# Modulation columns of a hybrid attention, SSD and convolution kernel: from TensorE products over eight channel tiles to ScalarE products and GpSimd sums

## The chip, the core and the metric

The kernel runs on one core of a Trainium2 chip. Its metric is the time of one execution on the device in microseconds. A core has TensorE (PE in the rows; PEld are its weight loads), VectorE (DVE), ScalarE (ACT), GpSimd (POOL) and SyncE (SP), each with its own queue that runs in order, and 16 DMA engines.

## What is computed

Two layers of a diffusion backbone with 512 latent tokens and 256 context tokens of 1024 channels. Each layer normalizes its input and modulates it with a shift and a scale, projects it once for three branches (attention, a bidirectional state space scan, a convolution module), merges the branches and adds the result through a gate:

```python
mod = jax.nn.silu(c) @ w_mod + b_mod
mod_c = jax.nn.silu(c_ctx) @ w_mod + b_mod
shift, scale, gate = jnp.split(mod[:, None, :], 3, axis=-1)
shift_c, scale_c, gate_c = jnp.split(mod_c, 3, axis=-1)
h = rmsnorm(x, norm_w) * (1.0 + scale) + shift
hc = rmsnorm(xc, norm_w) * (1.0 + scale_c) + shift_c
...
x_new = x + gate * out
...
return x_new, xc + gate_c * out_c
```

The change is about `mod` and `mod_c`: for each layer a vector of 1024 inputs times a matrix of 1024 x 3072, for two inputs (`c` and `c_ctx`). The matrix is 12.6 MB in each layer.

## The kernel before

**Layout.** Channels lie on the 128 partitions, tokens along the free axis; the 1024 channels are 8 tiles of 128. The 3072 modulation columns of a layer are 24 tiles of 128, written `m0`: 0 to 7 shift, 8 to 15 scale, 16 to 23 gate. Products of large matrices are done in three passes (`mm_cm_steps`, L175, and `mm_tm`, L216 to L218): a weight tile `raw` is split by ScalarE into `whi` (L156) and by VectorE into `wlo` (L157), the input stands split as `hh` and `hl`, and TensorE adds hi x hi, hi x lo and lo x hi. Weights pass through a ring of three `raw` tiles and five halves each of `whi` and `wlo`; SP issues the loads.

**Order in a layer.** First the gated inputs of the convolution module (`ps_u`, `ps_g`), then the projections `kvd`, `xbc` (8 tiles, each with a short convolution of 5 taps on VectorE, `xacc`, L564 and L567), `z` and `q`. Beside these VectorE works through the long convolution: 4 channel tiles with 31 taps, 30 of them on VectorE (`vacc`, L445), each adding `vt` times a tap to the sum in place. After `q` stands `layer_norm`, whose transposes (`pt_ln`, L617) read the finished taps of all four channel tiles. Then come the projections `gcv`, the scan with the merge of branch 2 woven in, attention with the merge of branch 1 woven in, the merge of branch 0, and the output projection (`ps_o`). In layer 0 that projection ends with the normalization for layer 1, which needs layer 1's shift and scale.

**Who sets the order.** From `kvd` to the end of attention TensorE runs in the order in which the code is written (`manual_schedule`). The other engines, and TensorE elsewhere, run in an order that the framework's scheduler makes before the run. An engine executes its list strictly in order, and a wait holds up all that stands behind it.

**The modulation.** The 16 column tiles of shift and scale of layer 0 come first (`mod_tiles`, L229) and are not touched. The remaining 32 (gate of layer 0 in the `xbc` stage, all of layer 1 in the three merges of layer 0) go through `Mods.visit` and `mod_half`. One visit treats 4 column tiles and half of the 8 channel tiles: two loads of 512 KB into the ring of weights, and 16 matmuls with the two input vectors as a stationary operand of 32 columns, the four column tiles in four column groups of the array:

```python
T.matmul(ps[32 * j:32 * j + 32, 0:P], sc[:, 4 * half + i, :], raws[i // 2][:, j, i % 2, :],
         start=(i == 0), stop=(i == 3), tile_position=(0, 32 * j))
```

The first half's result is copied out by ScalarE, the second half's is added by VectorE (L262), and a transpose on TensorE (L266) and an addition of the bias (L267) bring it into `mod`. `then` places the transpose about 12288 columns of matmul later.

Of the kernel before, what the change touches and what calls it, by code (L numbers as in the profile page):

```python
# [9 lines left out]
F32 = mybir.dt.float32  # L10
F32R = mybir.dt.float32r
AF = mybir.ActivationFunctionType
ALU = mybir.AluOpType
# [37 lines left out]
MOD_LAG = 12288  # L51
# [6 lines left out]
def hybrid_kernel(ctx, tc, xT, cc, consts, rope, mod_params, params, fnw, w_mod, w_cm, w_q, w_kvd, w_z,  # L58
# [71 lines left out]
    V.memset(nhalf, -0.5)  # L130

# [112 lines left out]
    def mod_half(li, mod, m0, half, part):  # L244


        raws = []
        for i in range(2):
            raw = wp.tile([P, 4, 2, P], F32, tag="raw", name="raw")
            k0 = 4 * half + 2 * i  # L250
            with tc.high_priority(offset=TOP):
                nc.sync.dma_start(raw, w_mod[li, m0:m0 + 4, :, k0:k0 + 2, :].rearrange("m p k c -> p m k c"))
            raws.append(raw)
        ps = pot("ps_mod")
        for i in range(4):
            for j in range(4):
                T.matmul(ps[32 * j:32 * j + 32, 0:P], sc[:, 4 * half + i, :], raws[i // 2][:, j, i % 2, :],
                         start=(i == 0), stop=(i == 3), tile_position=(0, 32 * j))
        if half == 0:
            S.activation(part, ps[:, 0:P], AF.Copy)  # L260
            return None
        V.tensor_tensor(out=part, in0=ps[:, 0:P], in1=part, op=ALU.add)  # L262

        def finish():
            pt = ps[:, P:2 * P]
            T.transpose(pt, part, ident)  # L266
            V.tensor_tensor(  # L267
                out=mod[:, m0:m0 + 4, :], in0=pt.rearrange("p (j r) -> p j r", j=4)[:, :, 0:2],
                in1=pmod[:, li, O_BMOD + m0:O_BMOD + m0 + 4].unsqueeze(2).to_broadcast([P, 4, 2]), op=ALU.add)

        return finish

    class Mods:


        def __init__(self, li, mod, m0):
            self.li, self.mod, self.m0, self.n = li, mod, m0, 0

        def visit(self):
            g, half = divmod(self.n, 2)  # L280
            if half == 0:
                self.part = sm.tile([P, P], F32, tag="part", name="part4")
            self.n += 1
            return mod_half(self.li, self.mod, self.m0 + 4 * g, half, self.part)
# [88 lines left out]
    for li in range(2):  # L373
# [168 lines left out]
        for ct in range(8):  # L542
# [15 lines left out]
            if li == 0 and ct % 2 == 1:  # L558
                fn = gate_mods.visit()
                if fn is not None:  # L560
                    soon.append(fn)
# [762 lines left out]
```

## Time and profile before

| what | value |
|---|---|
| time, median of 3 runs | 1486.73 us (1482.37 to 1487.7) |
| the profiled execution, its own time | 1484.83 us |
| its span in the trace | 1483.0 us |
| TensorE busy | 1441.4 us, 97% of the span |
| VectorE busy | 1038.6 us, 70% |
| ScalarE busy | 714.9 us, 48% |
| GpSimd busy | 80.4 us, 5% |
| mean granted TensorE clock, share of full | 0.994 |

Matmuls overlap in the pipeline, so a busy TensorE is counted from the start of the first to the end of the last, and distances of starts tell what one costs. VectorE's rows overlap a little too: an instruction is counted until its result is written. Busy shares are means over stages with different limits.

### The profile page before, as it was taken

How to read it: one execution, taken by the hardware profiler on the slowest of the kernel's cores; microseconds unless marked ns; L12 is line 12 of the kernel's file. 1: busy time of each engine (PE TensorE's matmuls, PEld its weight loads, DVE VectorE, ACT ScalarE, POOL GpSimd, SP SyncE). 2: the span in 40 equal slices, each digit the busy share in tenths (PEclk: the TensorE clock that was granted, in tenths of full speed). 3: DMA queues.
4: the chain of work that ended last, by engine and by line, in shares of the span. 5: the costliest groups of instructions: out<-in, count | busy, mean ns of one | idle time of the engine just before them, and what ended most of it. 6: DMA issues, size and time to landing. Idle time of an engine off the chain costs nothing.

```text
span 1483.0 us, 24837 instructions
## 1 busy us (share of the span) xinstructions
PE 1441.4 (97%) x9660; PEld 1251.2 (84%) x9660; DVE 1038.6 (70%) x1895; ACT 714.9 (48%) x1600; POOL 80.4 (5%) x177
## 2 busy tenths in 40 slices
PE   6999999999998999999999999999999999999997
PEld 5899899988887888888788888989988887888796
DVE  5689998766657776555444478899877788666564
ACT  5423543365444466556322344454464647666341
POOL 0000010100001210000000000001010121000000
PEclk9999999999999999999999999999999999999999
DMA  9223333223334323323554433223423242222551
GB/s 377 75 70 95 105 124 111 75 61 100 101 114 133 120 86 120 108 68 118 199 168 156 164 117 113 69 66 114 142 70 114 96 155 86 98 90 79 171 171 58
DMA packets 79671, 172.58 MB, mean 116 GB/s; under 512 B 7616, under 2 KB 37440, under 8 KB 79552
## 3 DMA queue, kind: packets, MB, share of 16 engines
q1 hardware_dynamic: 79552, 170.98, 35.1%
q8 instruction: 76, 1.25, 0.4%
q14 instruction: 43, 0.35, 0.1%
HBM read 143.43 MB, written 27.53 MB: 115 GB/s over the span
## 4 chain that ended last, share of the span: by engine, by line
PE 90%; DMA 3%; ACT 3%; DVE 2%; issue 1%; SPq 0%; POOL 0%; POOLq 0%; DVEq 0%; ACTq 0%
PE ps_gm L175 22%; PE ps_br L175 11%; PE ps_xbc L175 8%; PE ps_o L175 6%; PE ps_gcv L175 4%; PE ps_u L175 4%; PE ps_g L175 4%; PE po_v L1088 3%; PE ps_ga L175 3%; PE pt_p L1074 3%; PE ps_l L1028 2%; PE ps_z L216 1%; PE ps_q L217 1%; PE ps_z L217 1%; PE ps_q L216 1%; PE ps_z L218 1%
## 5 line engine op out<-in xcount | busy, mean ns | idle before, releaser
L156 ACT ACTIVATE whi<-raw 128x512 fp32r<-128x512 f32 (+1 forms) x316 | 198.7, 632 | 270.6 <-PE ps_gm L175 59.1
L157 DVE TENSOR_TENSOR wlo<-raw,whi 128x512 fp32r<-128x512 f32 (+1 forms) x316 | 217.2, 691 | 147.5 <-ACT whi L156 137.7
L445 DVE SCALAR_TENSOR_TENSOR vacc<-vt,par,vacc 128x783 f32<-128x783 f32 (+1 forms) x232 | 206.7, 891 | 8.9 <-ACT vacc L442 5.4
L175 PE MATMUL ps_gm<-hh,whi 128*128 128x512 f32 (+1 forms) x576 | 212.1, 368 | 0.0
L175 PE MATMUL ps_gm<-hh,wlo 128*128 128x512 f32 (+1 forms) x576 | 209.7, 364 | 0.0
L175 PE MATMUL ps_gm<-hl,whi 128*128 128x512 f32 (+1 forms) x576 | 209.0, 363 | 0.0
L175 PEld LDWEIGHTS ps_gm<-hh,wlo 128*128 128x128 f32 x576 | 109.0, 189 | 15.9 <-issue 2.1
L175 PEld LDWEIGHTS ps_gm<-hh,whi 128*128 128x128 f32 x576 | 109.1, 189 | 15.5 <-issue 2.0
L175 PEld LDWEIGHTS ps_gm<-hl,whi 128*128 128x128 f32 x576 | 108.9, 189 | 14.2 <-issue 1.0
L175 PE MATMUL ps_xbc<-hh,whi 128*128 128x512 f32 (+1 forms) x240 | 83.4, 348 | 0.0
L175 PE MATMUL ps_xbc<-hl,whi 128*128 128x512 f32 (+1 forms) x240 | 82.3, 343 | 0.0
L175 PE MATMUL ps_xbc<-hh,wlo 128*128 128x512 f32 (+1 forms) x240 | 82.3, 343 | 0.0
L1080 ACT ACTIVATE pth<-pt_p 128x512 f32<-128x512 f32 x72 | 43.5, 604 | 55.5 <-PE pt_p L1074 55.3
L698 ACT ACTIVATE tg<-ps_gm,hw 128x512 f32<-128x512 f32 x72 | 44.3, 615 | 47.6 <-PE ps_gm L175 46.5
L175 PE MATMUL ps_o<-yh,whi 128*128 128x256 f32 (+1 forms) x208 | 65.8, 318 | 0.5 <-DVE xnew L1153 0.3
L175 PE MATMUL ps_o<-yh,wlo 128*128 128x256 f32 (+1 forms) x208 | 65.7, 316 | 0.0
L175 PE MATMUL ps_o<-yl,whi 128*128 128x256 f32 (+1 forms) x208 | 65.7, 316 | 0.0
L1034 DVE TENSOR_REDUCE mx<-ps_l 128x1 f32<-128x512 f32 x64 | 43.9, 689 | 30.1 <-PE ps_l L1028 29.6
L567 DVE SCALAR_TENSOR_TENSOR xacc<-xraw,par,xacc 128x770 f32<-128x770 f32 (+1 forms) x64 | 62.7, 989 | 1.7 <-ACT xacc L564 1.5
L728 DVE SCALAR_TENSOR_TENSOR tg<-tg,ps_br 128x512 f32<-128x512 f32 x66 | 39.5, 599 | 32.7 <-PE ps_br L175 28.6
L1074 PE MATMUL pt_p<-mr,pe 128*128 128x128 f32 x416 | 62.3, 272 | 0.0
L1074 PEld LDWEIGHTS pt_p<-mr,pe 128*128 128x128 f32 x416 | 50.7, 140 | 10.5 <-issue 0.2
(281 smaller groups left out, 3635.7 us busy)
## 6 DMA issues: line engine op xcount, KB each, us to landing
raw<-in_w_cm_dram SPq DMA_DIRECT2D x96, 512.0 KB, 3.6
raw<-in_w_mod_dram SPq DMA_DIRECT2D x32, 512.0 KB, 5.2
raw<-in_w_br_dram SPq DMA_DIRECT2D x24, 512.0 KB, 3.7
raw<-in_w_out_dram SPq DMA_DIRECT2D x21, 512.0 KB, 3.8
wm<-in_w_mod_dram SPq DMA_DIRECT2D x16, 512.0 KB, 9.0
ydr<-tg SPq DMA_DIRECT2D x16, 384.0 KB, 3.0
yo<-ydr SPq DMA_DIRECT2D x16, 384.0 KB, 3.2
raw<-in_w_z_dram SPq DMA_DIRECT2D x8, 512.0 KB, 3.8
```

What stands on the lines that cost most here:

```text
L156: S.activation(hi, raw[:, u0:u0 + m, :], AF.Copy)
L157: V.tensor_tensor(out=lo, in0=raw[:, u0:u0 + m, :], in1=f(hi), op=ALU.subtract)
L175: T.matmul(ps[:, :b - a], st[:, col], mv(k)[:, a:b], start=(n == 0), stop=(n == len(order) - 1))
L216: T.matmul(ps[:, :ncol], xh(k)[:, t], hi, start=(k == 0), stop=False)
L445: V.scalar_tensor_tensor(out=acc[:, :n] if j else vt[:, o:o + n], in0=vt[:, o + j:o + j + n], scalar=cw(j), in1=acc[:, :n], op0=ALU.mult, ...
L567: xm = V.scalar_tensor_tensor(out=acc[:, :n], in0=raw[:, j:j + n], scalar=par[:, O_SCW + ct * 5 + j:O_SCW + ct * 5 + j + 1], in1=acc[:, :n ...
L698: lambda ps, a, b: S.activation(tg[:, a:b], ps, AF.Tanh, scale=0.5, bias=hw[:, br * 8 + ct:br * 8 + ct + 1]), "ps_gm")
L728: V.scalar_tensor_tensor(out=tg[:, a:b], in0=tg[:, a:b], scalar=1.0, in1=ps, op0=ALU.add, op1=ALU.mult)
L1034: V.tensor_reduce(out=mx[:, 0, j:j + 1], in_=pl[j], axis=AX.X, op=ALU.max, negate=True)
L1074: T.transpose(pt[:, tok(2 * i + j)], pes[j][:, tok(k1 + i)], ident)
L1080: S.activation(pf, pt, AF.Copy)
L1088: T.matmul(po[64 * j:64 * j + 64, 0:P], vv[:, k0 + k1 + i, g, :], pth[:, i, j, :], start=(k1 + i == 0), stop=(k1 + i == nk - 1), tile_posi ...
```

## The change

The column tiles after the first 16 are computed in another way, still 4 at a time. A `feed` takes one of the 8 channel tiles: a load of 256 KB, two multiplications on ScalarE by the two input values of each partition (into `mprod` for `c`, in place in `mraw` for `c_ctx`), and, from the second channel tile on, two additions on GpSimd into the sums of the first. After 8 feeds a `turn` adds the 128 partitions up on TensorE with 8 matmuls whose stationary operand `pick` has a single column of ones, and a second `turn` transposes as before. The pieces stand in the small buffers (tag `W2`, seven of them, of up to 512 values a partition), which they share with `kv`, `zs`, `qv` and others, not in the ring of weights. The gate columns of layer 1 move from the merge of branch 2 in layer 0 to layer 1's own `xbc` and `z` stages; shift and scale of layer 1 move to the merge of branch 0 and the output projection of layer 0. `na` no longer has a tile of its own.

```diff
+    pick = const.tile([P, 33], F32, name="pick")
+    V.memset(pick, 0.0)
+    V.memset(pick[:, 1:2], 1.0)
...
-    def mod_half(li, mod, m0, half, part):
...
     class Mods:
...
-        def __init__(self, li, mod, m0):
-            self.li, self.mod, self.m0, self.n = li, mod, m0, 0
...
+        def __init__(self, groups):
+            self.groups, self.n, self.ready, self.last = groups, 0, [], None
+
+        def feed(self):
+            g, k = divmod(self.n, KD)
+            if g >= len(self.groups):
+                return
             self.n += 1
-            return mod_half(self.li, self.mod, self.m0 + 4 * g, half, self.part)
+            li, m0 = self.groups[g]
+            p1 = small([P, 4, P], F32, "mraw")
+            nc.sync.dma_start(p1, w_mod[li, m0:m0 + 4, :, k, :].rearrange("m p c -> p m c"))
+            p0 = small([P, 4, P], F32, "mprod")
+            S.activation(p0, p1, AF.Copy, scale=sc[:, k, 0:1])
+            S.activation(p1, p1, AF.Copy, scale=sc[:, k, 1:2])
+            if k == 0:
+                self.acc = p0, p1
+            else:
+                for acc, p in zip(self.acc, (p0, p1)):
+                    G.tensor_tensor(out=acc, in0=acc, in1=p, op=ALU.add)
+            if k == KD - 1:
+                self.ready.append((li, m0, self.acc))
+
+        def turn(self):
+
+            if self.last is not None:
...
+            elif self.ready:
+                li, m0, acc = self.ready.pop(0)
+                ps = pot("ps_mod")
+                for r in range(2):
+                    for j in range(4):
+                        T.matmul(ps[32 * j:32 * j + 32, 0:P], pick[:, 1 - r:33 - r], acc[r][:, j, :], start=(r == 0),
+                                 stop=(r == 1), tile_position=(0, 32 * j))
+                part = sm.tile([P, P], F32, tag="part", name="part4")
+                S.activation(part, ps[:, 0:P], AF.Copy)
+                self.last = li, m0, ps, part
...
-        gate_mods = Mods(0, mods[0], 16)
+        gate_mods = Mods([(li, 16), (li, 20)])
...
-            if li == 0 and ct % 2 == 1:
-                fn = gate_mods.visit()
-                if fn is not None:
-                    soon.append(fn)
+            gate_mods.feed()
...
+                gate_mods.feed()
+                if b == 0 and tt in (2, 3):
+                    gate_mods.turn()
                 conv(2, xm)
...
+                if b == 1 and tt in (0, 2):
+                    gate_mods.turn()
                 conv(2, xm)
...
+        md = Mods([] if last else [(1, m0) for m0 in (0, 4, 8, 12)])
...
-                if not last and ct % 2 == 1:
-                    end = next_mods.visit()
-                    yield 2048
-            if end is not None:
-                end()
-
-        merge_cols = KD * (36 * ntok + (0 if last else 1024))
+                if fin:
+                    if ct in (4, 5, 7):
+                        md.turn()
+                    for _ in range(3):
+                        md.feed()
+
+        merge_cols = KD * 36 * ntok
...
             for ct in range(OUT_FIRST):
                 out_tile(ct, (lat, cx))
+                md.turn()
+                for _ in range(4):
+                    md.feed()
...
             for ct in range(OUT_FIRST, KD):
                 out_tile(ct, (lat,))
+                if ct > OUT_FIRST:
+                    md.turn()
                 add(lat_rms, ct)
```

TensorE, in layer 0 between the second and the third tile of `xbc`, before: `ps_xbc` is the bank of the projection, `ps_mod` that of the modulation.

```order
L175 MATMUL ps_xbc<-hl,whi 128x256
L175 MATMUL ps_xbc<-hh,wlo 128x256
L257 MATMUL ps_mod<-raw,sc 32x128 x16
L175 MATMUL ps_xbc<-hh,whi 128x512
L175 MATMUL ps_xbc<-hl,whi 128x512
```

With the change no modulation matmul stands in the `xbc` stage; the first turn of the layer stands between two tiles of `z`:

```order
L219 MATMUL ps_z<-wlo,hh 128x256
L220 MATMUL ps_z<-whi,hl 128x256
L290 MATMUL ps_mod<-mprod,pick 32x128 x4
L290 MATMUL ps_mod<-mraw,pick 32x128 x4
L218 MATMUL ps_z<-whi,hh 128x256
```

Four visits of 16 matmuls have become two turns of 8 in this layer.

GpSimd, at the beginning of the `xbc` stage of layer 0, before: it only zeroes the padding of the tiles `xraw` of the short convolution.

```order
L546 MEMSET xraw_1336 128x2
L547 MEMSET xraw_1336 128x2
L549 MEMSET xraw_1336 128x2
L546 MEMSET xraw_1412 128x2
L547 MEMSET xraw_1412 128x2
```

The same place with the change:

```order
L559 MEMSET xraw_1338 128x2
L271 TENSOR_TENSOR mprod_1396<-mprod_1396,mprod_1479 128x512
L271 TENSOR_TENSOR mraw_1394<-mraw_1394,mraw_1477 128x512
L271 TENSOR_TENSOR mprod_1396<-mprod_1396,mprod_1574 128x512
L556 MEMSET xraw_1419 128x2
L557 MEMSET xraw_1419 128x2
L559 MEMSET xraw_1419 128x2
L271 TENSOR_TENSOR mraw_1394<-mraw_1394,mraw_1572 128x512
L271 TENSOR_TENSOR mprod_1396<-mprod_1396,mprod_1669 128x512
```

The additions stand between the zeroings and ahead of those of later tiles: of the 14 additions of the first group 13 stand ahead of the zeroing for the third `xbc` tile.

ScalarE, among the tiles of `z` in layer 0, before: `zs` is the eviction of a bank of `z`, `bc` and `bt` belong to the scan's inputs.

```order
L588 ACTIVATE zs_2131<-ps_z_2106 128x256
L588 ACTIVATE zs_2167<-ps_z_2142 128x256
L538 ACTIVATE bt_1325<-pt_x_2170 128x512
L538 ACTIVATE bt_1325<-pt_x_2176 128x256
L588 ACTIVATE zs_2207<-ps_z_2182 128x256
```

With the change:

```order
L595 ACTIVATE zs_2181<-ps_z_2156 128x256
L293 ACTIVATE part4_2200<-ps_mod_2191 128x128
L580 ACTIVATE bc_1324<-xacc_2041 128x512
L582 ACTIVATE bc_1324<-xacc_2041 128x256
L265 ACTIVATE mprod_2186<-mraw_2184,sc_93 128x512
L266 ACTIVATE mraw_2184<-mraw_2184,sc_93 128x512
L595 ACTIVATE zs_2229<-ps_z_2204 128x256
L265 ACTIVATE mprod_2234<-mraw_2232,sc_93 128x512
L266 ACTIVATE mraw_2232<-mraw_2232,sc_93 128x512
L595 ACTIVATE zs_2268<-ps_z_2243 128x256
```

Two multiplications of a piece now stand ahead of each of these evictions.

## Rows read from the trace of the kernel before

**Rows 1.** The page: busy us by engine with instructions, and the chain's shares.

```profile
PE 1441.4 (97%) x9660; PEld 1251.2 (84%) x9660; DVE 1038.6 (70%) x1895; ACT 714.9 (48%) x1600; POOL 80.4 (5%) x177
...
PE 90%; DMA 3%; ACT 3%; DVE 2%; issue 1%; SPq 0%; POOL 0%; POOLq 0%; DVEq 0%; ACTq 0%
```

**Rows 2.** Busy us by stretch: length, PE, PEld, DVE, ACT, POOL; granted clock, DMA share, GB/s.

```profile
124.00:271.00 147.00, 145.91 (x1139) 136.07 (x1138) 133.74 (x170) 61.05 (x119) 8.42 (x28) 1.00 0.34 111
905.00:1076.00 171.00, 168.60 (x1072) 152.86 (x1071) 154.36 (x242) 78.82 (x155) 7.57 (x26) 0.99 0.32 100
717.00:866.00 149.00, 148.86 (x916) 125.94 (x912) 68.03 (x102) 48.11 (x78) 0.00 (x0) 1.00 0.53 174
```

**Rows 3.** Timeline (start, us): last tap and first layer norm transposes, both layers.

```profile
265.44 1.03 DVE L445 SCALAR_TENSOR_TENSOR vt<-vt,par,vacc 128x783 f32<-128x783 f32 x1
...
270.71 0.60 PE L617 MATMUL pt_ln<-mr,vt 128*128 128x128 f32 x4
...
1070.90 0.75 DVE L445 SCALAR_TENSOR_TENSOR vt<-vt,par,vacc 128x512 f32<-128x512 f32 x1
...
1075.76 0.60 PE L617 MATMUL pt_ln<-mr,vt 128*128 128x128 f32 x4
```

**Rows 4.** VectorE's costliest groups from 124 to 271 us: busy, mean ns, idle before.

```profile
L445 DVE SCALAR_TENSOR_TENSOR vacc<-vt,par,vacc 128x783 f32<-128x783 f32 x76 | 78.3, 1031 | 2.3 <-ACT vacc L442 1.1
L567 DVE SCALAR_TENSOR_TENSOR xacc<-xraw,par,xacc 128x770 f32<-128x770 f32 x32 | 32.7, 1031 | 0.7 <-ACT xacc L564 0.7
L157 DVE TENSOR_TENSOR wlo<-raw,whi 128x512 fp32r<-128x512 f32 x34 | 23.1, 688 | 9.5 <-ACT whi L156 9.3
```

**Rows 5.** The modulation's bank: records of L257, ns min/median/max, first and last start.

```profile
L257 PE MATMUL ps_mod<-raw,sc x512: 272/273/298, 140.5 to 782.0; 128*32 128x128 f32 x171
```

**Rows 6.** TensorE's timeline around the first visit of layer 0.

```profile
140.22 0.28 PE L175 MATMUL ps_xbc<-hl,whi 128*128 128x256 f32 x1
140.34 0.28 PE L175 MATMUL ps_xbc<-hh,wlo 128*128 128x256 f32 x1
140.55 1.08 PE L257 MATMUL ps_mod<-raw,sc 128*32 128x128 f32 x32
141.56 0.50 PE L175 MATMUL ps_xbc<-hh,whi 128*128 128x512 f32 x1
141.90 0.40 PE L175 MATMUL ps_xbc<-hl,whi 128*128 128x512 f32 x1
142.13 0.39 PE L175 MATMUL ps_xbc<-hh,wlo 128*128 128x512 f32 x1
```

**Rows 7.** TensorE's timeline around a piece of a visit in the last merge.

```profile
744.11 0.28 PE L175 MATMUL ps_br<-ua,wlo 128*128 128x256 f32 x1
744.32 0.64 PE L257 MATMUL ps_mod<-raw,sc 128*32 128x128 f32 x16
744.89 0.50 PE L175 MATMUL ps_gm<-hh,whi 128*128 128x512 f32 x1
```

**Rows 8.** TensorE's timeline at a transpose that waited (idle before it, releaser).

```profile
450.28 0.33 PE L266 MATMUL ps_mod<-mr,part 128*128 128x128 f32 x1 [1.25 <-DVE part L262]
```

**Rows 9.** ScalarE's groups: the weight split, 128x512.

```profile
L156 ACT ACTIVATE whi<-raw 128x512 fp32r<-128x512 f32 x308 | 193.4, 631 | 262.0 <-PE ps_gm L175 59.1 <-DMA raw<-in_w_cm_dram 54.4 <-PE ps_o L175 30.0
```

**Rows 10.** Timelines: table products on GpSimd, VectorE beside them; last a product alone.

```profile
206.28 1.01 DVE L567 SCALAR_TENSOR_TENSOR xacc<-xraw,par,xacc 128x770 f32<-128x770 f32 x1
...
207.38 1.46 POOL L386 TENSOR_TENSOR cwq<-rt,par 128x256 f32<-128x256 f32 x1 [20.71 <-DMA rt<-in_rope_dram]
...
208.16 1.50 DVE L567 SCALAR_TENSOR_TENSOR xacc<-xraw,par,xacc 128x770 f32<-128x770 f32 x1
...
266.55 0.73 POOL L386 TENSOR_TENSOR ktab<-rt,par 128x256 f32<-128x256 f32 x1 [53.56 <-DVE vt L445]
267.25 1.17 POOL L391 TENSOR_TENSOR ktab<-rt,par 128x64 f32<-128x64 f32 x4
...
1192.77 1.04 POOL L827 TENSOR_TENSOR y<-xt,par 128x512 f32<-128x512 f32 x1 [9.26 <-issue]
```

More of the change, by code (lines that the diff above doesn't have):

```diff
@@ L50 @@
 PIECE = 1024
-MOD_LAG = 12288
 OUT_FIRST = 3
@@ L242, in mod_tiles @@
         return finish
-    def mod_half(li, mod, m0, half, part):
[L247 to L271, printed above, removed]
@@ L273, in hybrid_kernel @@
-    class Mods:
-        def __init__(self, li, mod, m0):
-            self.li, self.mod, self.m0, self.n = li, mod, m0, 0
[L279 to L282, printed above, removed]
-            self.n += 1
-            return mod_half(self.li, self.mod, self.m0 + 4 * g, half, self.part)
+    class Mods:
+        def __init__(self, groups):
[4 more added lines that the diff above has]
+                return
+            self.n += 1
+            li, m0 = self.groups[g]
[13 more added lines that the diff above has]
+            if self.last is not None:
+                li, m0, ps, part = self.last
+                self.last = None
+                pt = ps[:, P:2 * P]
+                T.transpose(pt, part, ident)
+                V.tensor_tensor(
+                    out=mods[li][:, m0:m0 + 4, :], in0=pt.rearrange("p (j r) -> p j r", j=4)[:, :, 0:2],
+                    in1=pmod[:, li, O_BMOD + m0:O_BMOD + m0 + 4].unsqueeze(2).to_broadcast([P, 4, 2]), op=ALU.add)
+            elif self.ready:
[8 more added lines that the diff above has]
+                self.last = li, m0, ps, part
@@ L485, in hybrid_kernel @@
         man.__enter__()
-        na = sm.tile([P, 16], F32, tag="na", name="na")
-        S.activation(na, par[:, O_AL:O_AL + 16], AF.Exp)
+        na = par[:, O_AL:O_AL + 16]
+        S.activation(na, na, AF.Exp)
         V.tensor_scalar(out=na, in0=na, scalar1=-1.0, scalar2=None, op0=ALU.mult)
@@ L681, in hybrid_kernel @@
         yh, yl = [], []
-        def then(fn, steps):
-            done = 0
-            for n in steps:
-                yield n
-                done += n
-                if done >= MOD_LAG and fn is not None:
-                    fn()
-                    fn = None
-            if fn is not None:
-                fn()
+        md = Mods([] if last else [(1, m0) for m0 in (0, 4, 8, 12)])
         def sig_steps(br, ct, tg):
@@ L712, in merge_steps @@
                 yl.extend([yb[:, i, :] for i in range(4)] + [work([P, ntok], F32R, "yl") for _ in range(4)])
-            end = None
-            next_mods = Mods(1, mods[1], 8 * (2, 1, 0)[br])
             for ct in range(KD):
@@ L733, in merge_steps @@
                 else:
-                    yield from then(end, sig_steps(br, ct, tg))
-                    end = None
-                yield from then(end, mm_cm_steps(wb, lambda k: u[0][:, k, :], lambda k: u[1][:, k, :], ntok, br_out,
-                                                 "ps_br", slice(c0, c0 + P)))
-                end = None
+                    yield from sig_steps(br, ct, tg)
+                yield from mm_cm_steps(wb, lambda k: u[0][:, k, :], lambda k: u[1][:, k, :], ntok, br_out,
+                                       "ps_br", slice(c0, c0 + P))
                 if not first:
```

## The prediction

> **What bounds the kernel now.** I read the page first: TensorE is busy for 1441.4 of 1483.0 us, and the chain that ended last runs over it for 90% [rows 1]. So a microsecond of TensorE work that goes is a microsecond of time, unless another engine makes TensorE wait in that stage. Which stages are close to that, the busy times by stage tell [rows 2]. In the two stretches that end with the layer norms (124 to 271 us in layer 0, 905 to 1076 us in layer 1) VectorE is busy 133.7 of 147 us and 154.4 of 171 us, each over 90%; in the last merge and the output projection of layer 0 (717 to 866 us) it is busy 68 of 149 us. Then the places where TensorE meets VectorE: the last convolution tap ends at 265.44 + 1.03 = 266.5 us and the first layer norm transpose, which needs all taps, starts at 270.71 us; in layer 1 it is 1071.65 and 1075.76 us [rows 3]. VectorE is done 4.2 and 4.1 us before TensorE needs it: these stretches have two bounds side by side, with 4 us between them. Last, what VectorE does there: taps, the short convolution and weight splits, 76, 32 and 34 instructions that read two tensors of SBUF, 134 us together [rows 4], as much as its busy time there.
>
> **The change, part by part.**
>
> *Matmuls removed.* The trace has 512 records of L257, two for each of 256 matmuls, 32 for each of 16 visits [rows 5]. One visit: the last matmul ahead of it starts at 140.34, the visit at 140.55, the next matmul at 141.56 and the one after that at 141.90 [rows 6]. That is 1.56 us; without the visit those steps take 0.12 (256 columns) and 0.23 (512 columns, 141.90 to 142.13). A visit costs 1.21 us, 16 cost 19.4 us.
>
> *Matmuls added.* A turn has 8 matmuls of the same shape, 16 records. Before, a piece of 16 records went from 744.32 to 744.89 us, entered 0.21 us after the last start ahead of it (0.12 without it) [rows 7]; the matmul after it I let take 0.11 us longer, as after the visit: 0.57 + 0.20 = 0.77 us, 8 turns 6.2 us. The 8 transposes stay. Two losses go: the 1.25 us in which TensorE waited for the addition of the two halves at 450.28 [rows 8], and the cuts in the last merge, where the 4 visits stand in 11 pieces; 7 entries more at 0.20 are 1.4 us. TensorE alone gets back 19.4 + 1.25 + 1.4 - 6.2 = 16 us. Of that, 4 visits and 2 turns lie ahead of the layer norm in layer 0 and 2 turns ahead of it in layer 1. Where VectorE sets the end these count for nothing, so the gain in the other stages is 12 x 1.21 + 1.25 + 1.4 - 4 x 0.77 = 14 us.
>
> *ScalarE.* 64 pieces get two multiplications of 128x512, SBUF to SBUF. The nearest row, the weight split of that shape, takes 0.63 us [rows 9]: 20 us in each of the two gate stretches, 40 us in 717 to 866. ScalarE is busy there 61 of 147, 79 of 171 and 48 of 149 us [rows 2], which hides them. Below 0 they cannot be; if a multiplication waits for its piece or for a free small buffer, what stands behind it on ScalarE are evictions of TensorE's banks, and then TensorE waits. I take 0, and up to 8 us in 717 to 866.
>
> *GpSimd, the disputed part.* 8 groups have 7 x 2 additions: 28 in each gate stretch, 56 in 717 to 866. An addition of 128x512 with two full inputs is not in the trace. Below it stands the one with a per-head factor, 1.04 us alone; above it a line through the table products, 128x64 in 1.17/4 = 0.29 and 128x256 in 0.73 us when VectorE is idle, gives 0.73 + 256 x 2.3 ns = 1.3 us [rows 10]. What it does to VectorE is in the same rows: the 128x256 product beside the taps takes 1.46 instead of 0.73 us, it had to wait; and the convolution step that came next took 1.50 instead of 1.01 us, so it waited for GpSimd. VectorE lost 0.49 us to a product of 0.73 us, all but 0.24. For the new additions that makes 1.04 - 0.24 = 0.80 to 1.3 - 0.24 = 1.06 us each; I take 0.95, since their inputs are full as those of the line are. The Trainium skill has the rule in "SBUF — State Buffer", "Who interferes with whom": a VectorE instruction with two SBUF inputs and a GpSimd instruction that reads SBUF need the same read interface, and the second to come waits until the first has finished. The rows agree in kind; for a lock over the whole instruction they fall 0.24 us short, and with the whole instruction held the sum would be 56 x 0.9 x 0.24 = 12 us higher than mine.
>
> In the gate stretches VectorE is busy 0.91 and 0.90 of the time, all of it with such instructions, so an addition that starts meets one nine times in ten: 28 x 0.95 x 0.9 = 24 us more on VectorE in each. From that go the 4.2 and 4.1 us between the bounds, and what VectorE's own idle time takes up: 13.3 us without the 4.2 leave 9.1 in layer 0, 16.6 without 4.1 leave 12.5 in layer 1. In layer 0 it is mostly waits for ScalarE's half of a weight split, 9.3 of 13.3 us [rows 4]; ScalarE gets its buffers from TensorE, so these waits move along in part when TensorE is late, and I let half of the idle time be taken up. Layer norm late by 24 - 4.2 - 4.5 = 15 us in layer 0, by 24 - 4.1 - 6 = 14 us in layer 1. What is late next is all of TensorE: nothing stands ahead of those transposes in its written order that could fill the gap. In 717 to 866 VectorE is under half busy, has no such edge, and I charge nothing: 56 additions at 1.3 us are 73 of 149 us on GpSimd.
>
> *What moves on queues.* The zeroing of the padding of the third and later tiles stands behind the additions on GpSimd now. At about 0.95 us of its own and one VectorE instruction of waiting each, 14 additions take some 28 us; VectorE is later than that anyway. The pieces' DMAs, 64 for 32 with the same bytes, stand on SP ahead of weights and wait for small buffers; the DMA share of 0.3 to 0.5 [rows 2] leaves room, and I price the waiting as a rival.
>
> *Sum.* 1484.83 us, this execution's own time, + 15 + 14 - 14 = 1500 us. The median of the runs shown lies 1.9 us above this execution; I say 1501.
>
> **Rivals.**
>
> 1. *The additions are hidden and TensorE's gain stands.* For it speaks that 13 to 17 us of VectorE's time in each stretch are idle and that GpSimd is idle nearly throughout; against it that most of the idle time is waits for ScalarE between two instructions, and that the bulk of VectorE's work there reads two tensors of SBUF. Then all 16 us are gained: 1484.8 - 16 = 1469. It decides from 13 us of lost VectorE time per stretch in layer 0, 16 in layer 1 downward, that is from about 0.5 us per addition.
> 2. *The small buffers run short.* Two sums hold two of seven buffers for eight pieces, and the evictions of z come from the same seven. In the z tiles one piece is multiplied per tile; a tile is 24 steps of 0.12 = 2.9 us, two additions with a tap between them 2 x (0.95 + 0.94) = 3.8 us. If evictions wait for GpSimd, that is 0.9 x 8 = 7 us per layer on top of the forecast: 1515. Against it: most of this delay passes while VectorE is late anyway.
> 3. *The two bounds meet.* With 0.80 us per addition and all idle time taken up the layer norms are late by 28 x 0.80 x 0.9 = 20 less 13.3 and 16.6, so 7 and 4 us: 1484.8 + 11 - 14 = 1482. No difference that can be told.
>
> **How the numbers follow.** Chances: forecast 0.60, rival 1 0.18, rival 2 0.13, rival 3 0.09. The forecast's own range is 1492 (0.80 us and half the idle time, 20 - 8.7 = 11 and 20 - 10.1 = 10 us) to 1521 (1.06 us, no idle time taken up, 27 - 4 = 23 and 23 us, 1484.8 + 46 - 14 = 1517, and some of the 8 us). Since rival 1 holds nearly two in ten, the range reaches towards it: 1472 to 1521. This kernel's measurement tells about 0.5%, 7.4 us, from no change. Rival 1 is faster by more (0.18); rival 3 and the lower edge of the forecast are within (0.12); the rest is slower (0.70).
>
> **What would show it.** If right: L445 and the short convolution have instructions of about 2 us beside additions of L271; VectorE's time in them grows by some 24 us in each stretch; TensorE idles ahead of the layer norm transposes or for evictions before them, and the layer norms start near 285 us and, in layer 1, some 15 us later than the output projection ahead of it would let them; the stages between are shorter by 14 us. Wrong would be: taps that keep their 1.03 us, or a layer norm that starts ahead of 271 us.

## The result and the profile after

The changed kernel took 1536.57 us (median of 4 runs, 1535.51 to 1538.41), the kernel before 1486.99 us beside it: ratio 1.034, 95% interval 1.0322 to 1.0358. It is slower, as forecast, but by 50 us and not by some 15; the forecast range ended at 1521 us. The profiled execution took 1535.51 us with a span of 1533.7 us, 50.7 us more than the span before.

The page of the changed kernel first, busy time by engine and the chain:

```profile
PE 1450.9 (95%) x9276; PEld 1255.5 (82%) x9276; DVE 1115.4 (73%) x1889; ACT 791.5 (52%) x1728; POOL 262.9 (17%) x289
...
PE 74%; DVE 11%; issue 5%; ACT 5%; DMA 4%; POOL 1%; SPq 0%; POOLq 0%; DVEq 0%; ACTq 0%
...
L271 POOL TENSOR_TENSOR mprod<-mprod 128x512 f32<-128x512 f32 x56 | 91.2, 1629 | 356.8 <-ACT mprod L265 263.4
```

TensorE's share of the chain fell from 90% [rows 1] to 74%; VectorE, ScalarE and transfers came in. Now the same stretches as in [rows 2], which end at the layer norms and at the first sum of squares of the output projection, with the columns of that group:

```profile
123.00:297.00 174.00, 152.33 (x1043) 139.47 (x1043) 160.95 (x169) 79.87 (x151) 57.20 (x59) 0.95 0.30 94
929.00:1128.00 199.00, 180.62 (x1105) 161.32 (x1104) 182.26 (x244) 97.35 (x189) 53.09 (x57) 0.94 0.34 107
732.00:890.00 158.00, 150.76 (x860) 127.38 (x859) 91.34 (x108) 87.28 (x143) 86.00 (x56) 0.98 0.59 188
```

They are 27, 28 and 9 us longer. The points in time that the tables below go by are the first and last starts of two of TensorE's tiles: the layer norm's transposes (layer 0, layer 1) and the sums of squares in the output projection of layer 0, here with the change and, in the last row, the sums of squares before:

```profile
L627 PE MATMUL pt_ln<-mr,vt x24: 270/273/273, 296.7 to 313.2; 128*128 128x128 f32 x24
...
L627 PE MATMUL pt_ln<-mr,vt x16: 270/272/273, 1127.8 to 1137.7; 128*128 128x128 f32 x16
...
L328 PE MATMUL ps_ss<-cst,sq x12: 165/251/251, 889.7 to 917.7; 128*128 128x2 f32 x12
...
L318 PE MATMUL ps_ss<-cst,sq x12: 165/251/251, 865.8 to 893.9; 128*128 128x2 f32 x12
```

The layer norms began at 270.7 and 1075.8 us before [rows 3]. So the span's 50.7 us split in this way; the 28 us between the first and the last sum of squares are the same in both and left out. The table of the experiments uses the first three columns:

| us | start to first layer norm | from there to the first sum of squares | last sum of squares to second layer norm | rest |
|---|---|---|---|---|
| before | 270.7 | 595.1 | 181.9 | 407.2 |
| after | 296.7 | 593.0 | 210.1 | 405.9 |
| difference | +26.0 | -2.1 | +28.2 | -1.3 |
| forecast | +15 | -14 (with the rest) | +14 | |

VectorE's groups in the first stretch, beside [rows 4], and what GpSimd's additions and the taps do to each other where nothing else runs (timeline of GpSimd, then of VectorE):

```profile
L455 DVE SCALAR_TENSOR_TENSOR vacc<-vt,par,vacc 128x783 f32<-128x783 f32 x77 | 93.6, 1215 | 2.1 <-ACT vacc L452 1.1
L574 DVE SCALAR_TENSOR_TENSOR xacc<-xraw,par,xacc 128x770 f32<-128x770 f32 x32 | 34.9, 1098 | 0.2
L159 DVE TENSOR_TENSOR wlo<-raw,whi 128x512 fp32r<-128x512 f32 x34 | 29.3, 877 | 7.4 <-ACT whi L158 7.2
```

```profile
226.95 2.03 POOL L271 TENSOR_TENSOR mraw<-mraw 128x512 f32<-128x512 f32 x1
228.94 2.02 POOL L271 TENSOR_TENSOR mprod<-mprod 128x512 f32<-128x512 f32 x1
230.92 2.02 POOL L271 TENSOR_TENSOR mraw<-mraw 128x512 f32<-128x512 f32 x1
...
227.85 7.91 DVE L455 SCALAR_TENSOR_TENSOR vacc<-vt,par,vacc 128x783 f32<-128x783 f32 x4
```

The two engines take strict turns: one tap and one addition every 1.98 us (7.91/4). Taps alone start 1.07 us apart (four starts from 283.09 to 286.30), additions alone 1.25 us (736.18 and 737.43).

How that gets to TensorE shows in the waits of ScalarE and of TensorE, 123 to 297 us (total, number, longest), and in the timelines of ScalarE, GpSimd and TensorE in the short convolutions:

```profile
ACT mprod L265 <- DMA mraw<-in_w_mod_dram: 15.0, 9, 4.2
ACT xcm L580 <- DVE xacc L574: 14.9, 2, 7.7
...
PE pt_x L547 <- ACT xcm L580: 7.3, 2, 6.9
PE ps_xbc L177 <- ACT xraw L561: 5.6, 6, 2.8
PE ps_z L219 <- DVE wlo L159: 4.6, 2, 2.6
PE pt_x L547 <- ACT bc L580: 2.5, 1, 2.5
```

```profile
141.17 0.72 ACT L265 ACTIVATE mprod<-mraw,sc 128x512 f32<-128x512 f32 x1 [4.21 <-DMA mraw<-in_w_mod_dram]
...
142.56 0.58 ACT L561 ACTIVATE xraw<-ps_xbc 128x512 f32<-128x512 f32 x1
143.31 1.29 POOL L271 TENSOR_TENSOR mraw<-mraw 128x512 f32<-128x512 f32 x1
...
158.07 0.63 ACT L580 ACTIVATE xcm<-xacc 128x512 f32<-128x512 f32 x1 [7.74 <-DVE xacc L574]
...
158.75 1.54 PE L547 MATMUL pt_x<-mr,xcm 128*128 128x128 f32 x6 [6.88 <-ACT xcm L580]
```

ScalarE stands 4.21 us before a multiplication whose piece has not come, with the eviction of TensorE's bank (L561) behind it; later it stands 7.74 us before the SiLU. The four steps of that short convolution, with the taps and small steps between them, take VectorE from 143.3 to 158.0 us, 14.7 us where it was 8.4 before (133.9 to 142.3), and TensorE stands 6.88 us for that SiLU. All waits of TensorE in this stretch sum to 21.6 us; before there was a single one, 1.1 us for ScalarE, and none for VectorE.

### The profile page after: what moved, and what is told of

Its sections match the earlier page's. It is cut to its first block, busy times and chain, and to the rows that moved or that the text cites. A ratio compares the mean times of both kernels' runs of the same rounds, so it can differ in the third digit from the quotient of the medians.

```text
span 1533.7 us, 24539 instructions
## 1 busy us (share of the span) xinstructions
PE 1450.9 (95%) x9276; PEld 1255.5 (82%) x9276; DVE 1115.4 (73%) x1889; ACT 791.5 (52%) x1728; POOL 262.9 (17%) x289
## 4 chain that ended last, share of the span: by engine, by line
PE 74%; DVE 11%; issue 5%; ACT 5%; DMA 4%; POOL 1%; SPq 0%; POOLq 0%; DVEq 0%; ACTq 0%
PE ps_gm L177 19%; PE ps_br L177 9%; PE ps_o L177 7%; DVE vacc L455 4%; PE ps_gcv L177 4%; PE ps_xbc L177 4%; PE ps_u L177 4%; PE ps_g L177 3%; PE ps_ga L177 3%; PE po_v L1086 3%; PE pt_p L1072 3%; DMA mraw<-in_w_mod_dram 2%; PE ps_l L1026 2%; DVE wlo L159 2%; DVE xacc L574 2%
## 5 line engine op out<-in xcount | busy, mean ns | idle before, releaser
L159 DVE TENSOR_TENSOR wlo<-raw,whi 128x512 fp32r<-128x512 f32 (+1 forms) x316 | 243.0, 774 | 126.8 <-ACT whi L158 116.4
L455 DVE SCALAR_TENSOR_TENSOR vacc<-vt,par,vacc 128x783 f32<-128x783 f32 (+1 forms) x232 | 233.8, 1008 | 7.6 <-ACT vacc L452 4.2
L271 POOL TENSOR_TENSOR mprod<-mprod 128x512 f32<-128x512 f32 x56 | 91.2, 1629 | 356.8 <-ACT mprod L265 263.4
L177 PE MATMUL ps_xbc<-hh,whi 128*128 128x512 f32 (+1 forms) x240 | 86.5, 361 | 9.0 <-ACT xraw L561 9.0
L271 POOL TENSOR_TENSOR mraw<-mraw 128x512 f32<-128x512 f32 x56 | 91.7, 1638 | 2.9 <-ACT mraw L266 2.2
L265 ACT ACTIVATE mprod<-mraw,sc 128x512 f32<-128x512 f32 x64 | 46.2, 721 | 65.8 <-DMA mraw<-in_w_mod_dram 57.4
L574 DVE SCALAR_TENSOR_TENSOR xacc<-xraw,par,xacc 128x770 f32<-128x770 f32 (+1 forms) x64 | 67.1, 1056 | 0.7 <-ACT xacc L571 0.5
```

Of the source, the lines that this page charges most:

```text
L159: V.tensor_tensor(out=lo, in0=raw[:, u0:u0 + m, :], in1=f(hi), op=ALU.subtract)
L177: T.matmul(ps[:, :b - a], st[:, col], mv(k)[:, a:b], start=(n == 0), stop=(n == len(order) - 1))
L265: S.activation(p0, p1, AF.Copy, scale=sc[:, k, 0:1])
L271: G.tensor_tensor(out=acc, in0=acc, in1=p, op=ALU.add)
L455: V.scalar_tensor_tensor(out=acc[:, :n] if j else vt[:, o:o + n], in0=vt[:, o + j:o + j + n], scalar=cw(j), in1=acc[:, :n], op0=ALU.mult, ...
L574: xm = V.scalar_tensor_tensor(out=acc[:, :n], in0=raw[:, j:j + n], scalar=par[:, O_SCW + ct * 5 + j:O_SCW + ct * 5 + j + 1], in1=acc[:, :n ...
```

## The experiments

All kernels were timed against the kernel before on the same chip. "LN0" is the first column of the table above, "out" the second, "LN1" the third.

| kernel | us | ratio (95%) | LN0 | out | LN1 |
|---|---|---|---|---|---|
| before | 1487 | | 270.7 | 595.1 | 181.9 |
| after | 1536.6 | 1.034 (1.0322 to 1.0358) | 296.7 | 593.0 | 210.1 |
| e1 no additions | 1483.1 | 0.9974 (0.9961 to 0.9988) | 273.0 | 585.7 | 188.0 |
| e2 one input | 1505.0 | 1.0131 (1.0113 to 1.015) | 284.5 | 586.7 | 197.4 |
| e3 on VectorE | 1514.7 | 1.0202 (1.0185 to 1.022) | 282.7 | 594.2 | 196.5 |
| e4 gates only | 1529.7 | 1.0297 (1.0282 to 1.0312) | 297.6 | 588.8 | 209.0 |
| e5 shift and scale only | 1481.3 | 0.9956 (0.9942 to 0.9971) | 272.7 | 590.2 | 182.2 |
| e6 sums elsewhere | 1529.3 | 1.0295 (1.0257 to 1.0333) | 290.7 | 593.6 | 209.5 |
| e7 two merges, GpSimd | 1512.8 | 1.018 (1.0157 to 1.0204) | 270.1 | 623.5 | 181.9 |
| e8 two merges, fused | 1498.2 | 1.009 (1.0056 to 1.0125) | 270.6 | 606.3 | 182.2 |
| e9 half the additions | 1503.6 | 1.0113 (1.0091 to 1.0135) | 282.4 | 590.9 | 194.5 |
| e10 zeroing on VectorE | 1530.9 | 1.0306 (1.0285 to 1.0326) | 293.4 | 591.8 | 207.4 |
| e11 last merge, fused | 1482.1 | 0.9972 (0.9961 to 0.9983) | 270.3 | 592.4 | 182.0 |
| e12 last merge, VectorE adds | 1481.9 | 0.9971 (0.9957 to 0.9985) | 270.4 | 592.8 | 181.9 |
| e13 no multiplications | 1473.1 | 0.9913 (0.9898 to 0.9927) | 273.0 | 581.6 | 182.2 |
| e14 no pieces | 1474.0 | 0.9919 (0.9905 to 0.9934) | 272.5 | 582.3 | 182.1 |
| e15 shift and scale, fused | 1475.8 | 0.993 (0.9916 to 0.9944) | 269.7 | 587.1 | 182.2 |

**e1: no additions.**

```diff
-            else:
-                for acc, p in zip(self.acc, (p0, p1)):
-                    G.tensor_tensor(out=acc, in0=acc, in1=p, op=ALU.add)
```

> The 112 additions on GpSimd are left out (each sum is only its first piece's product, so the modulation of these columns is not the reference's); pieces, ScalarE's multiplications, the turns on TensorE and their places stay. Theory A (GpSimd's additions hold up VectorE's two-input instructions, and what ScalarE and TensorE get from VectorE comes late): all of the loss goes and TensorE's 16 us are gained, 1467 to 1478 us, first layer norm at 265 to 272 us. Theory B (ScalarE waits for pieces that wait for small buffers, which the additions hold): also back, since the buffers come free at once, 1470 to 1485. Theory C (the loss lies in the other parts: 64 pieces of 512-byte runs, 128 multiplications, turns): stays above 1515 us.

1483.1 us: the additions, and what hangs on them, are 53 us of time. The time lies above theory A's range and inside theory B's, so this run alone does not choose between the two; e2, e3 and e6 bear on that. It takes theory C out for the loss against before, but not altogether: only 3 us were gained where TensorE's sum gives 16. Something else in the change costs some 13 us, which no theory here covered (e13).

**e2: one input, and e3: the additions on VectorE.**

```diff
-                for acc, p in zip(self.acc, (p0, p1)):
-                    G.tensor_tensor(out=acc, in0=acc, in1=p, op=ALU.add)
+                for p in (p0, p1):
+                    G.tensor_scalar(out=p, in0=p, scalar1=1.0, scalar2=None, op0=ALU.mult)
```

> Each addition on GpSimd becomes a multiplication of the same 128x512 piece by 1.0, which reads one tensor (the sums are again only the first product, so the modulation is not the reference's). GpSimd's queue, the order, and how the buffers are held stay. Theory A, if only two-input instructions of GpSimd shut VectorE out: taps beside them keep 1.03 us, 1468 to 1485 us. Theory B (buffers and queues): the pieces are held about as long, 1510 to 1535 us. If a one-input instruction shuts VectorE out as well, taps of some 2 us stay and the time is above 1515.

1505.0 us, outside of what any of the three cases gave. The timelines of GpSimd and VectorE say why:

```profile
222.53 1.49 POOL L271 TENSOR_SCALAR mraw<-mraw 128x512 f32<-128x512 f32 x1
223.99 1.49 POOL L271 TENSOR_SCALAR mprod<-mprod 128x512 f32<-128x512 f32 x1
...
221.08 5.81 DVE L455 SCALAR_TENSOR_TENSOR vacc<-vt,par,vacc 128x783 f32<-128x783 f32 x4
```

An instruction of GpSimd with one input takes 1.49 us, longer than the addition, and a tap beside it 1.45 us (5.81/4): it costs VectorE 0.4 us, where an addition costs it 0.9 in the same place. So it does shut VectorE out, for a part. GpSimd was busy about as long (58.0 us from 123 to 285 us, against 57.2 from 123 to 297 us in the whole change), so the pieces were held about as long, and buffers and GpSimd's queue alone can't be what makes 1536.6.

e3 is `V.tensor_tensor` in place of `G.tensor_tensor`.

> The additions run on VectorE in GpSimd's place; all else stays. Theory A: an addition then takes VectorE 0.69 us (as the weight split of that shape) and not the 1.0 us that it loses beside GpSimd, 28 x 0.3 = 8 us less in each gate stretch and some 4 us less in the last merge: 1510 to 1522 us; the first layer norm at 286 to 291 us. Theory B (GpSimd's own queue and speed hold the buffers): 1480 to 1500 us, since the pieces are freed in 0.7 us each.

1514.7 us, as theory A said and above theory B's 1480 to 1500: 22 us less than with GpSimd, although VectorE now does the work itself. Its groups show an addition at 0.69 us, and taps at their old length:

```profile
L455 DVE SCALAR_TENSOR_TENSOR vacc<-vt,par,vacc 128x783 f32<-128x783 f32 x77 | 79.3, 1030 | 2.0 <-ACT vacc L452 1.1
...
L271 DVE TENSOR_TENSOR mprod<-mprod 128x512 f32<-128x512 f32 x14 | 9.7, 693 | 4.4 <-ACT mprod L265 4.4
```

LN0 came at 282.7, 3 us sooner than expected; some taps now stood behind its first transposes, and the transposes after those waited 7.0 us for the last of them, which falls into the second column.

**e4 and e5: one part alone.** In e4 only the gate columns take the new way, in e5 only the 16 shift and scale columns; the others are visited as before.

```diff
 (e4, against before)
-        gate_mods = Mods(0, mods[0], 16)
+        gate_mods = Feeds([(li, 16), (li, 20)])
...
-                if not last and ct % 2 == 1:
+                if not last and br > 0 and ct % 2 == 1:
                     end = next_mods.visit()
 (e5, against before)
+        md = Feeds([] if last else [(1, m0) for m0 in (0, 4, 8, 12)])
...
-                if not last and ct % 2 == 1:
+                if not last and br == 0 and ct % 2 == 1:
                     end = next_mods.visit()
```

> Only the gate columns take the new way (2 groups in each layer's stretch ahead of the layer norm); the 16 shift and scale columns of layer 1 are visited as before in the first two merges. If the loss is where the trace shows the layer norms late: the first at 297 us, the second 28 us late on top, so 54 us lost and 6 us regained in the last merge (4 visits, 7 cuts): 1530 to 1540 us. If the two parts hurt each other, below 1520 us.

> Only the 16 shift and scale columns of layer 1 take the new way, in the last merge and the output projection of layer 0; the gate columns are visited as before (4 visits among the short convolution's tiles, 4 in the last merge). Theory A: the first layer norm is back at 271 us; 8 visits and the stall go ahead of 717 us (11 us gained), and 56 additions in the last merge cost what they cost in the whole change, 8 us net of 6 us that are not regained here: 14 us. Sum 1488, within 1484 to 1493 us. If the parts act on each other: below 1480 or above 1500.

1529.7 and 1481.3 us, the first just under its range: the loss lies in the gate columns, in the two stretches ahead of the layer norms (LN0 +27, LN1 +27). The other part alone is 6 us faster than before, 3 us beyond the expected edge. The two differences, +43 and -6, sum to 37 and not to the whole change's 50. Some 8 of these 12 us are in the last merge, from the attention's last value matmul to the first sum of squares. Before the change layer 1's gate columns stood in this merge, that of branch 0, and not in that of branch 2. The stretch takes 149 us before, 142 in e4, 156 in e5 and 157 in the whole change, although e5 still has the four gate visits (6 us) there. With GpSimd's additions TensorE's sum no longer sets it, and what is taken from TensorE gives nothing back.

**e6: the running sums elsewhere, e10: the zeroing on VectorE.**

```diff
 (e6)
+            own = k == 0 and m0 >= 16
-            p0 = small([P, 4, P], F32, "mprod")
+            p0 = fill([P, 4, P], "macc") if own else small([P, 4, P], F32, "mprod")
+            q1 = fill([P, 4, P], "macc") if own else p1
...
 (e10)
-            G.memset(raw[:, 0:2], 0.0)
...
+            V.memset(raw[:, 0:2], 0.0)
...
```

> As the whole change, but the two running sums of a gate group stand in buffers that are idle in that stretch, so that all seven small buffers are left for pieces, products and evictions. Theory A (VectorE shut out by GpSimd): no change by more than 5 us, 1530 to 1540 us, first layer norm at 293 to 299 us. Theory B (small buffers run short): 10 us or more come back in each gate stretch, below 1518 us.

> The zeroing of the short convolution's padding goes from GpSimd, where it stands behind additions, to VectorE; all else is the whole change. Theory A: 1530 to 1542 us, since VectorE is the one that is full. Theory D (the third tile's zeroing is late behind 13 additions and holds ScalarE's eviction and TensorE): 10 us or more come back, below 1526 us.

1529.3 and 1530.9 us. Two more small buffers bring LN0 6 us forward, a little more than theory A said and less than the 10 of theory B, and LN1 by less than 1 us; the zeroing gives 3 us in each layer, inside theory A's range. Both are side costs of 6 to 7 us, not the cause.

**e9: half of the additions.** Only one of the two sums is added up.

> Only one of the two running sums of each group is added up (56 additions instead of 112; the other sum stays its first product, so the second modulation vector is not the reference's). Pieces, multiplications, turns stay. Theory A with every microsecond that VectorE loses handed on: half of the 53 us between no additions (1483) and all of them (1536.6): 1505 to 1515 us, first layer norm at 282 to 288 us. If VectorE's idle time and the lead of the last tap take up the first part of the loss: 1486 to 1500 us, first layer norm below 280 us.

1503.6 us, between the two expectations: of the 53 us, the first half of the additions costs 20 and the second 33. Against e1, LN0 is 9.4 us later with the first 14 additions of its stretch and another 14.3 us with the next 14, LN1 6.5 and 15.6 us (22.1 in all). Some 5 to 9 us of the loss are taken up, the rest goes straight through.

**e13 and e14: what is left without additions.** e13 is e1 with ScalarE multiplying a group's first piece only; e14 leaves the other pieces' transfers out too.

```diff
-            p0 = small([P, 4, P], F32, "mprod")
-            S.activation(p0, p1, AF.Copy, scale=sc[:, k, 0:1])
-            S.activation(p1, p1, AF.Copy, scale=sc[:, k, 1:2])
             if k == 0:
+                p0 = small([P, 4, P], F32, "mprod")
+                S.activation(p0, p1, AF.Copy, scale=sc[:, k, 0:1])
+                S.activation(p1, p1, AF.Copy, scale=sc[:, k, 1:2])
                 self.acc = p0, p1
```

> Additions left out, and of ScalarE's 128 multiplications only the 16 of each group's first piece stay (the modulation of these columns is not the reference's); the pieces still come, nothing reads seven of eight. Without additions the kernel took 1483 us, not the 1469 that TensorE's gain would give; the layer norms stood at 273.0 us and 6 us late in layer 1, and the last merge gained nothing. Theory S (ScalarE, in order, waits for pieces with evictions and weight splits behind it): 1468 to 1475 us, first layer norm at 266 to 271 us. Theory P (the pieces' transfers, ahead of weights on SP's queue): still 1480 to 1486. Theory V (VectorE's own work sets the layer norms, so nothing can be gained there): 1474 to 1480, first layer norm at 270 to 273 us.

> As the one before, and the transfers of seven of eight pieces are left out too (again not the reference's modulation): what is left of the change is the visits taken away and the turns put in. Theory P: 1468 to 1475 us, 8 us or more below the kernel with the transfers. Theory S: within 3 us of it. Theory V: 1472 to 1480 us with the first layer norm at 270 us or later.

1473.1 and 1474.0 us: the times are those of theory S, and the transfers cost nothing. Without ScalarE's multiplications 10 us are gone, 6 of them in LN1 and 4 in the second column (3 in the last merge). As the products' small buffers go with them, no run here tells the work on ScalarE from the buffers that it holds. In e1, between 887 and 1075 us and between 709 and 859 us, ScalarE stood for them this long, with evictions and weight splits behind it:

```profile
ACT mprod L265 <- DMA mraw<-in_w_mod_dram: 11.6, 8, 2.4
...
ACT mprod L265 <- DMA mraw<-in_w_mod_dram: 19.5, 12, 5.9
```

LN0 stayed at 273.0 with and without them, where theory S had 266 to 271, and 2 us later than before although four visits are gone. That is what theory V gave for this stretch: what is taken from TensorE there gives nothing back. That VectorE's order sets it is not shown beyond this, and why it is 2 us worse was not followed further.

**e7, e8, e11, e12, e15: versions that might beat both.** e7 feeds layer 1's 24 columns three pieces a tile in the second and the last merge, with additions on GpSimd. e8 is the same with multiplication and addition in one instruction of VectorE, and ScalarE multiplying a group's first piece only:

```diff
-                for acc, p in zip(self.acc, (p0, p1)):
-                    G.tensor_tensor(out=acc, in0=acc, in1=p, op=ALU.add)
+                for r, acc in enumerate(self.acc):
+                    V.scalar_tensor_tensor(out=acc, in0=p1, scalar=sc[:, k, r:r + 1], in1=acc, op0=ALU.mult, op1=ALU.add)
...
```

> A version that could beat both: layer 0's gate columns as before; the 24 columns of layer 1 the new way, with three pieces for each of the eight tiles of the second and of the last merge of layer 0, where VectorE is about two thirds busy. TensorE gains 12 visits, the stall and the cuts less 6 turns: 12.5 us. Theory A with the price of the last merge (56 additions cost 12 us, 0.22 us each): 84 additions cost 18 us, 1490 us, within 1482 to 1498. If additions are free where VectorE has room: 1472 us.

> As the kernel with three pieces per tile of the last two merges, but VectorE multiplies and adds in one instruction, 84 of about 0.7 us, without GpSimd, and ScalarE multiplies only the first piece of a group. Theory A: VectorE spends 59 us in some 340 us in which it has over 100 us idle, and nothing waits for GpSimd: 1472 to 1482 us, faster than before. If VectorE's late instructions hold TensorE in the attention as they did among the short convolutions: 1486 to 1495.

1512.8 and 1498.2 us, both above every case of their expectations. The second merge is woven into the attention, and there TensorE waits above all for copies of the transposed probabilities (`pth`), which stand on VectorE and ScalarE beside the new work (e7, then e8, 525 to 830 us; with the whole change TensorE's waits from 525 to 732 us were 0.4 us):

```profile
PE po_v L1145 <- DVE pth L1135: 9.4, 1, 9.4
PE po_v L1145 <- ACT pth L1137: 8.9, 8, 5.3
```

```profile
PE po_v L1145 <- DVE pth L1135: 5.9, 2, 5.1
PE ps_l L1085 <- ACT pe L1107: 3.7, 3, 1.4
```

VectorE's idle third there was not free time; that it is the gaps of a chain is a reading of these waits, and no run tests it.

e11 and e12 move only the shift and scale columns to the last merge, with layer 1's gate visits in the first merge; e11 with the fused instruction, e12 with ScalarE's multiplications and additions on VectorE. e15 is e5 with the fused instruction.

> A version that could beat both: gate columns as before (layer 1's four visits go to the first merge), the 16 shift and scale columns in the last merge and the output projection of layer 0, with multiplication and addition in one instruction of VectorE, no GpSimd, and ScalarE in the first piece of a group only. Four visits of the second merge go (5 us), four of the last merge and 7 cuts (6 us), 4 turns come (3 us). If neither VectorE (half idle there) nor ScalarE's waits for pieces cost anything: 1477 us. With the 4 us that the stretch loses without any addition: 1481. If VectorE's instructions wait for pieces and hold the weight splits: 1485 or more.

> The same as the fused version, but ScalarE multiplies every piece and VectorE only adds (56 additions of 0.69 us). The stretch from the last value matmul of the attention to the first sum of squares took 150.0 us with VectorE's additions in the whole change: 1486 - 5 + 1 = 1482 us, within 1478 to 1486. More than 2 us above the fused version would say that ScalarE's waits for pieces are a cost of their own.

> A version that could beat both: the shift and scale columns of layer 1 alone (1481.3 us with GpSimd's additions: 12 us gained ahead of 717 us, 7 lost behind), with multiplication and addition in one instruction of VectorE. The stretch behind the attention took 146.2 us in the fused version without gate visits and 156.1 here with GpSimd and four gate visits (6 us): about 152, so 4 us less: 1477 us, within 1474 to 1481. If the gate visits are what stretches that stretch: 1480 or more.

e11 and e12 took 1482.1 and 1481.9 us, so no difference between them and no more than e5 gave. The two bear on ScalarE as well: from the attention's end to the first sum of squares it waited 21.8 us for pieces in e12 and 5.0 in e11, and the stretch took 146.4 and 146.2 us. So in the last merge these waits can cost nothing, although e13 was 3 us shorter there than e1; what makes the difference is open. e15 took 1475.8 us, as expected, ratio 0.993 (0.9916 to 0.9944): 11 us faster than before, the fastest kernel here of those that leave nothing out. Its accumulations take VectorE 0.75 us, and GpSimd has nothing to do there (row of the accumulations, then the stretch from the attention's end to the first sum of squares, columns as in [rows 2]):

```profile
L314 DVE SCALAR_TENSOR_TENSOR mprod<-mraw,sc,mprod x28: 741/746/753, 705.4 to 820.6; 128x512 f32<-128x512 f32 x28
```

```profile
704.00:857.00 153.00, 149.67 (x968) 126.57 (x964) 103.03 (x165) 52.24 (x88) 0.00 (x0) 0.99 0.65 213
```

It is 153 us long; in e5 the same stretch took 156 us.

## Why the prediction was wrong

The mechanism of the loss was right: slower, by VectorE's turns with GpSimd, mostly ahead of the two layer norms. The size was off by 36 us: some 8 in what an addition costs VectorE, 17 in what was set off against it, and 11 in the last merge.

**What an addition costs VectorE: 24 us a stretch was too little, by 3 to 4.** The three groups above grew from 134 to 158 us against [rows 4], and the small steps of the softplus took a few more; summed over all instructions of VectorE beside an addition, over their undisturbed length, it is about 27.6 us in layer 0 and 28.1 in layer 1, so 0.99 us for each of 28 additions and not 0.95 x 0.9. Nothing escapes: each of the 28 additions of a stretch ran while VectorE had an instruction under way. The Trainium skill, "SBUF — State Buffer", "Who interferes with whom" and "Summary: rules for kernel authors", has the second engine wait for the whole instruction of the first. By that rule the prediction had 6 us more a stretch, 30 us, and a tap and an addition would take 2.3 us in series; the trace has 27.6 and 28.1 us, and 1.98 us a pair. So the lock is the right picture, less an overlap of 0.3 us, near the 0.24 that [rows 10] gave.

**The step that failed: "From that go the 4.2 and 4.1 us between the bounds".** I took the last tap and the layer norm as the edge where VectorE meets TensorE, so that TensorE would first use up the lead. VectorE's idle time up to the last tap was used up about as I let it, from 10.3 us (142.5 less 132.2 busy, 124 to 266.5 us) to 7.1 in layer 0, 3.2 us where I had 4.5, and the last tap came 23.0 us later. But the lead did not go; it grew. The stretch up to the last tap after, the tap itself, and the chain of layer 0 from VectorE to the layer norm:

```profile
123.00:289.50 166.50, 144.83 (x980) 131.97 (x980) 159.43 (x166) 77.12 (x145) 55.34 (x54) 0.95 0.31 96
```

```profile
288.46 1.03 DVE L455 SCALAR_TENSOR_TENSOR vt<-vt,par,vacc 128x783 f32<-128x783 f32 x1
```

```profile
263.18 0.61 DVE wlo L159
263.84 0.39 PE ps_q L219
...
296.88 0.44 PE pt_ln L627 x4
```

The taps were done at 289.5 us, 7.2 us ahead of the layer norm. What held TensorE last was a split of q's weights at 263.8 us, and from there it ran 33 us without a wait. VectorE works in order, so its loss enters TensorE at splits and short convolutions on the way, from 140 us on: TensorE's waits of 21.6 us in the stretch lie there, and none lies at the layer norm. Before, TensorE waited 1.1 us in the stretch, so its own work set the layer norm, and the 4.2 us were no store that a late VectorE would use up first. In e1, with no additions at all, the lead was 7.2 us as well; against e1 the layer norms are 23.7 and 22.1 us late, of VectorE's 27.6 and 28.1. That is 7 us of the error in layer 0 (4.2 counted, 3.0 grown) and 10 in layer 1 (4.1 counted, 6.2 grown: the last tap ended at 1117.4 us). Of these, 2 and 6 us are there in e1 already: the 6 are ScalarE's, which come next, and the 2 stay open.

**ScalarE at 0 and nothing charged in the last merge.** ScalarE's multiplications were priced at nothing for its idle time, with up to 8 us as an edge; by e13 against e1 they cost 10 us with the buffers that they hold: none in LN0, 6 in layer 1, 1 between the first layer norm and the attention's end, 3 in the last merge. With the additions on GpSimd the last merge loses more: from the attention's last value matmul to the first sum of squares it took 157 us for 149, where I had it some 3 us shorter. The chain there, 741 to 752 us, shows rival 2 in a place where I had not put it:

```profile
741.64 1.99 POOL mprod L271
743.63 5.23 DMA mraw<-in_w_mod_dram
...
748.95 0.73 ACT mprod L265
...
750.80 0.74 ACT ua L1135
751.54 0.02 issue
751.57 2.02 DVE ua L1136
```

An addition frees a buffer, the next piece's transfer starts, ScalarE waits for the piece in order, and what TensorE needs stands behind. In e3 and e12, where VectorE adds, the stretch took 150 and 146 us, so most of this is gone.

**What held.** From the first layer norm to the attention's last value matmul the kernel took 446.2 us before (to 716.9) and 435.8 after (to 732.5): 10.4 us came back for 8 visits and TensorE's one wait for the addition of two halves, priced at 10.9. Visits taken away ahead of the layer norm counted for nothing (LN0 of e13 and e14). Rivals 1 and 3 are out by e1 against the whole change; rival 2's buffers are a side cost of some 6 us in layer 0 (e6; that it lies in the z tiles is not shown), and its mechanism turned up in the last merge as well.

## What to carry to other kernels

Where VectorE is nine tenths busy with instructions that read two tensors of SBUF, an addition of two tensors given to GpSimd is not off VectorE's path: one of 128x512 cost VectorE 0.99 us, more than doing it there (0.69). A lead that one engine has over another at one place is slack only if nothing on the way ties the two together; follow the chain back to the last real wait before counting it. An engine half idle in a stretch is not for that reason free for work that waits in order for a transfer with evictions behind it: such work on ScalarE, with its buffers, cost 6 us ahead of the second layer norm here, and nothing in the last merge of e12. What it costs has to be read from its own stretch.

## What the runs showed of the hardware

A multiplication on GpSimd with one input took 1.49 us where the addition with two took 1.28, and taps beside it still started 1.45 us apart where taps alone start 1.07 apart.

TensorE's granted clock fell after it had idled: in these stretches of ten us (columns as above) it is 0.78 and 0.88 of full speed, and the matmuls from 161.06 to 162.34 us, behind the wait of 6.88 us, started 0.43 us apart where others of 512 columns start 0.23 apart (162.59 and 162.83 already do): 1.2 GHz for a while, the lower of its two levels, then 2.4.

```profile
150.00:160.00 10.00, 3.12 (x22) 2.81 (x21) 10.00 (x12) 2.26 (x5) 5.65 (x6) 0.78 0.17 54
160.00:170.00 10.00, 9.77 (x50) 8.10 (x48) 10.00 (x15) 2.83 (x7) 0.46 (x4) 0.88 0.15 52
```

```profile
161.06 0.63 PE L177 MATMUL ps_xbc<-hl,whi 128*128 128x512 f32 x1
161.49 0.63 PE L177 MATMUL ps_xbc<-hh,wlo 128*128 128x512 f32 x1
```

So these waits cost more than their length. Summed over steps that took about twice their usual distance with no wait ahead of them, it is an estimated 5 to 6 us in the first stretch and 10 in the second, a part of the 26 and 28.
